# A first projection in hand-written order: unnormalized x, the 1/rms applied at eviction, late constants

## The chip, the cores and the metric

The kernel runs on one core of a Trainium2 chip. The metric is device time in microseconds (us) of one execution; a profile of one further execution gives, for every instruction, its engine, start and duration. The engines are TensorE (PE in the rows; PEld is its weight load), VectorE (DVE), ScalarE (ACT), GpSimd (POOL) and the sync engine (SP), which issues most DMAs.

## The reference, cut to what matters

Two decoder layers over 256 tokens of width 1024. What the change touches is the head of the first layer:

```python
def rmsnorm(x, g):
    xf = x.astype(jnp.float32)
    y = xf * lax.rsqrt(jnp.mean(xf * xf, axis=-1, keepdims=True) + NORM_EPS)
    return (y * g.astype(jnp.float32)).astype(x.dtype)
...
    for layer in range(DEPTH):
        h = rmsnorm(x, pre_norm[layer])
        proj = h @ w_in[layer]
        (hq, hf, hi, hz, nq, kc, vc, ks, vs, kw, vw, ng, nz) = jnp.split(proj, offsets, axis=-1)
```

`nq` (1024 columns) gets a rotary embedding, `hf` (1024 columns) feeds the recurrent group, and the others follow. The rms factor is one number per token, so `(x * g) @ w` scaled by it afterwards gives the same projection.

## The kernel before, in words

All products are made in a split form: every fp32 operand is divided into a high part (a rounded copy, type fp32r) and a low part (the remainder), and one product is three matmuls: high by high, high by low, low by high. So each weight unit costs a ScalarE copy (`whi`, L202) and a VectorE subtraction (`wlo`, L203), both in `convert`, before TensorE may use it.

**The ring.** `plan` lists the weight units, 128 x 1024 numbers each (512 KB), in the order in which they are used: units 0 to 7 for `nq`, 8 to 15 for `hf`, 16 to 19 for `kc`/`vc`, 20 to 23 for `kw`/`vw`/gates (1072 wide), 24 to 27 for the first compressor, 28 to 31 for `ks`/`vs`. `Ring.fill` issues a unit's DMA on SP's queue (L226) into one of five raw buffers; a raw buffer is free again when both halves of the split have read it. Eight split units can be held. `done` releases a unit and fills again; with `lag` set, the conversion is put off by 9 us of a planned clock that `tick` advances with the matmuls.

**The order of work.** The kernel writes down instructions; a scheduler with a cost model then orders them on each engine, and each engine runs its own queue strictly in that order, waiting on semaphores. `later(lag, fn, channel)` plans a step behind the work in hand.

**The head of layer 0 (`layers`, L1075 to L1106).** SP issues the `pre_norm` row, x for tokens 0 to 127 (two halves), the constants table `ct` (identity, rope tables, masks), units 0 and 1, x for tokens 128 to 255, and further units. Four one-row matmuls (L1088) spread the `pre_norm` row over the partitions. `norm_in` squares and sums x (L339), makes 1/rms (L331, L332), multiplies x by it and by the weight (L344), transposes the result by eight TensorE transposes (L351), and splits it into `Hhi` and `Hlo` (L355, L356). Then `a_pair` makes the first projection: for token tile a = 0 and, four units later, for a = 1, six matmuls of 512 columns per unit and tile (`mm_a`, L368 to L370), 96 in all. `nq_evac` takes each finished bank through `rope` (L386 to L393), and 4 us of the planned clock later `turn_q` transposes it (L430) and splits it (L434, L435).

`consts2` loads the second table and six small tensors, clears buffers on GpSimd, transposes twice on TensorE (L293, L294) and makes `posh`, `posl`, `colT`, two masks and `lower_bound` (an exponential, L310) on VectorE and ScalarE. It is written ahead of the first projection.

**What follows.** `hgrn_fast` for c = 0, 1 makes the `hf` projection (`b_group`, `mm_b`, L378 to L380, whose moving operand spans both token tiles) and, behind it, two long scans per c on VectorE. `kcvc`, `kv_w` (whose gates take a sigmoid, L587), `compress` and `kv_s` come next. Three PSUM banks of tag `mm` serve all projections.

## Time and profile before

| | us |
|---|---|
| median of 3 runs | 558.88 (557.16 to 562.67) |
| the profiled execution | 558.97 |
| its span, first to last instruction | 557.2 |

The profile's page gives the busy time of each engine; the timeline lists instructions in order of time, start and duration in us, with the idle time ahead of one in brackets and what ended it; the groups by line give mean durations; the windows give busy time per stretch. PE busy includes time in which a matmul is in flight, so TensorE's rate is read from the steps between the starts of its matmuls.

### The profile page before, as it was taken

Reading aid. Unit: us, or ns where it says so; the run is one execution under the profiler, and the core shown is the slowest. Engines: PE = TensorE matmul, PEld = TensorE weight load, DVE = VectorE, ACT = ScalarE, POOL = GpSimd, SP = SyncE. Lnnn points to the kernel's source line nnn. Section 1 sums busy time; section 2 is a strip of 40 time slices with the busy share of each in tenths; the row PEclk is TensorE's granted clock in tenths of the full one; section 3 lists DMA queues with packets and bytes.
Section 4 is the critical chain, followed back from the end, with each engine's and each line's share of the span. In section 5 each row is a group of like instructions: output and inputs, shape, how many; then the busy total and the mean of one; then the engine's idle time right before and its main releaser. Section 6 shows DMA issues by size and latency. Waiting matters only on the chain.

```text
span 557.2 us, 9821 instructions
## 1 busy us (share of the span) xinstructions
PE 543.8 (98%) x3675; PEld 487.6 (88%) x3675; DVE 398.8 (72%) x883; ACT 333.0 (60%) x632; POOL 9.6 (2%) x18
## 2 busy tenths in 40 slices
PE   7999999999999999999999999989999999999994
PEld 4889998899888989988888999979988888898884
DVE  4887997889777277563687599888987654866422
ACT  6576537865567685562557763677646768746311
POOL 4000000000000001001000000000000000000000
PEclk9999999999999999999999999999999999999998
DMA  8698548965146158566385755697433622956111
GB/s 302 195 314 257 146 127 266 304 193 152 39 117 190 35 166 291 185 191 188 115 262 162 228 154 152 196 302 256 125 101 84 174 85 63 303 172 200 59 38 44
DMA packets 72197, 96.56 MB, mean 173 GB/s; under 512 B 3383, under 2 KB 49357, under 8 KB 72142
## 3 DMA queue, kind: packets, MB, share of 16 engines
q1 hardware_dynamic: 71854, 95.33, 55.2%
q8 instruction: 31, 0.51, 0.4%
q10 hardware_dynamic: 288, 0.52, 0.2%
q14 instruction: 24, 0.20, 0.1%
HBM read 93.75 MB, written 2.10 MB: 172 GB/s over the span
## 4 chain that ended last, share of the span: by engine, by line
PE 88%; DMA 4%; ACT 3%; DVE 2%; issue 1%; SPq 0%; ACTq 0%; DVEq 0%
PE ps_mm L378 10%; PE ps_mm L380 10%; PE ps_mm L379 10%; PE ps_mm L368 9%; PE ps_mm L369 9%; PE ps_mm L370 9%; PE ps_mm L1005 4%; PE ps_mm L1007 4%; PE ps_mm L1006 4%; DMA raw<-in_w_in 2%; ACT whi L202 2%; PE ps_t L668 2%; DMA raw<-in_cmp_w_v 2%; PE ps_s L608 1%; DVE wlo L203 1%
## 5 line engine op out<-in xcount | busy, mean ns | idle before, releaser
L203 DVE TENSOR_TENSOR wlo<-raw,whi 128x1024 fp32r<-128x1024 f32 (+1 forms) x168 | 203.0, 1223 | 60.7 <-ACT whi L202 56.3
L202 ACT CAST whi<-raw 128x1024 fp32r<-128x1024 f32 (+1 forms) x168 | 174.9, 1052 | 87.9 <-PE ps_mm L379 24.5
L378 PE MATMUL ps_mm<-Hhi,whi 128*128 128x256 f32 x448 | 127.5, 285 | 0.0
L380 PE MATMUL ps_mm<-Hhi,wlo 128*128 128x256 f32 x448 | 125.7, 281 | 0.0
L379 PE MATMUL ps_mm<-Hlo,whi 128*128 128x256 f32 x448 | 125.7, 281 | 0.0
L368 PE MATMUL ps_mm<-whi,Hhi 128*128 128x512 f32 (+1 forms) x256 | 102.0, 399 | 0.7 <-ACT Hhi L355 0.7
L370 PE MATMUL ps_mm<-whi,Hlo 128*128 128x512 f32 (+1 forms) x256 | 98.9, 386 | 0.0
L369 PE MATMUL ps_mm<-wlo,Hhi 128*128 128x512 f32 (+1 forms) x256 | 98.8, 386 | 0.0
L379 PEld LDWEIGHTS ps_mm<-Hlo,whi 128*128 128x128 f32 x448 | 84.5, 189 | 0.1
L378 PEld LDWEIGHTS ps_mm<-Hhi,whi 128*128 128x128 f32 x448 | 84.3, 188 | 0.1
L380 PEld LDWEIGHTS ps_mm<-Hhi,wlo 128*128 128x128 f32 x448 | 84.4, 188 | 0.0
L370 PEld LDWEIGHTS ps_mm<-whi,Hlo 128*128 128x128 f32 x256 | 48.7, 190 | 10.3 <-DVE Hlo L356 0.3
L368 PEld LDWEIGHTS ps_mm<-whi,Hhi 128*128 128x128 f32 x256 | 48.9, 191 | 8.5 <-ACT Hhi L355 1.1
L369 PEld LDWEIGHTS ps_mm<-wlo,Hhi 128*128 128x128 f32 x256 | 49.0, 191 | 7.5 <-DVE wlo L203 0.5
L630 ACT ACTIVATE sB<-ps_s,nm 128x256 f32<-128x256 f32 (+1 forms) x40 | 16.9, 428 | 12.2 <-DVE nm L627 11.5
L627 DVE CUSTOM_DVE_ANT_0 ps_s<-ps_s,cm 128x128 f32<-128x128 f32 (+1 forms) x64 | 22.4, 371 | 1.9 <-PE ps_s L610 0.7
L671 DVE TENSOR_TENSOR sB<-ps_t,sB 128x512 fp32r<-128x512 f32 x12 | 8.3, 688 | 20.1 <-ACT sB L670 20.1
L1005 PE MATMUL ps_mm<-whi,sN 128*128 128x512 f32 x48 | 19.0, 397 | 0.0
L1006 PE MATMUL ps_mm<-wlo,Hhi 128*128 128x512 f32 x48 | 18.9, 395 | 0.0
L1007 PE MATMUL ps_mm<-whi,Hlo 128*128 128x512 f32 x48 | 18.9, 395 | 0.0
L1006 PE MATMUL ps_mm<-wlo,sN 128*128 128x512 f32 x48 | 18.9, 394 | 0.0
L1007 PE MATMUL ps_mm<-whi,sN 128*128 128x512 f32 x48 | 18.9, 394 | 0.0
(299 smaller groups left out, 921.0 us busy)
## 6 DMA issues: line engine op xcount, KB each, us to landing
raw<-in_w_in SPq DMA_DIRECT2D x112, 512.0 KB, 4.5
raw<-in_w_out SPq DMA_DIRECT2D x32, 512.0 KB, 4.3
raw<-in_w_in SPq DMA_DIRECT2D x8, 536.0 KB, 4.1
raw<-in_cmp_w_k SPq DMA_DIRECT2D x16, 256.0 KB, 3.4
raw<-in_cmp_w_v SPq DMA_DIRECT2D x16, 256.0 KB, 3.2
sB<-in_x SPq DMA_DIRECT2D x3, 512.0 KB, 3.6
sB<-in_post_norm SPq DMA_DIRECT2D x2, 512.0 KB, 4.8
xs<-sB SPq DMA_DIRECT2D x4, 256.0 KB, 2.0
```

Source lines behind the costliest of these rows:

```text
L202: S.copy(out=hi, in_=raw)
L203: V.tensor_tensor(out=lo, in0=raw, in1=hi.bitcast(F32), op=OP.subtract)
L368: P.matmul(out=ps, lhsT=hh, rhs=wh, start=k == 0, stop=False)
L369: P.matmul(out=ps, lhsT=hh, rhs=wl, start=False, stop=False)
L370: P.matmul(out=ps, lhsT=hl, rhs=wh, start=False, stop=k == KT - 1)
L378: P.matmul(out=ps, lhsT=wh, rhs=hh, start=k == 0, stop=False)
L379: P.matmul(out=ps, lhsT=wh, rhs=hl, start=False, stop=False)
L380: P.matmul(out=ps, lhsT=wl, rhs=hh, start=False, stop=k == KT - 1)
L627: V.tensor_tensor_reduce(out=sb[b], in0=sb[b], in1=mk[b], scale=-1.0, scalar=3e38, op0=OP.add, op1=OP.min, accum_out=nm[:, i, b:b + 1])
L1005: P.matmul(out=ps, lhsT=hi, rhs=wh, start=first, stop=False)
L1006: P.matmul(out=ps, lhsT=hi, rhs=wl, start=False, stop=False)
L1007: P.matmul(out=ps, lhsT=lo, rhs=wh, start=False, stop=last)
```

## The change

The first projection of layer 0 is taken out of `norm_in` and `a_pair` and written as a function `first` inside a block in which the written order is each engine's order.

- x is transposed as it comes, without the norm. The transposes are multiplied by the `pre_norm` column (`whole`), split (`top`, `rest`), and used as the stationary operand of the 96 matmuls (`mm_x`). 1/rms goes into the rope tables and the scale of the eviction (`stats`, `evacuate`).
- For the later projections the normalized `Hhi` and `Hlo` are still needed: 1/rms is turned into a row by one matmul per token tile with a diagonal (`spread`), multiplied in (`product`) and split again (`normal`).
- Units are taken by both token tiles in turn; the weight splits of units 0 to 9 stand at written places, unit 0 in halves.
- Eight and two dummy matmuls of 384 columns (`dummies`) stand ahead of the first product.
- DMAs: the identity and the `pre_norm` column go on ScalarE's queue; SP issues x tile 0, unit 0 (two halves), x tile 1, units 1 and 2, the rest of the table, unit 3.
- `consts2` stands behind `hgrn_fast` for c = 1, with buffers of its own in place of shared ones; its clearing of buffers (`clear`) stays at the start.

```diff
         def convert(self, n):
             while len(self.split) < n:
-                raw, hi, lo, shaped = self.made[len(self.split)]
-                S.copy(out=hi, in_=raw)
-                V.tensor_tensor(out=lo, in0=raw, in1=hi.bitcast(F32), op=OP.subtract)
+                i = len(self.split)
+                if i >= self.early:
+                    self.high(i)
+                    self.low(i)
+                raw, hi, lo, shaped = self.made[i]
                 self.split.append((shaped(hi), shaped(lo)))
...
+    def mm_x(ps, un, u, H, order):
+        last = (u == KT // 2 - 1, order[-1], 1)
+        for j, kind in enumerate(order):
+            for i in range(2):
+                k = 2 * u + i
+                P.matmul(out=ps, lhsT=H[kind[0] == "l"][:, k, :], rhs=un[kind[1] == "l"][:, i, :],
+                         start=(u, j, i) == (0, 0, 0), stop=(True, kind, i) == last)
...
+    def first(ring, general):
...
+        def whole(a, k0, n):
+            ks, o = slice(k0, k0 + n), (k0 % 4) * 128
+            V.tensor_tensor(out=full[a][:, ks, :],
+                            in0=turned[a, k0 // 4][:, o:o + 128 * n].rearrange("p (k t) -> p k t", k=n),
+                            in1=gcol[:, ks, None].to_broadcast([128, n, 128]), op=OP.mult)
+
+        def top(a, k0, n):
+            S.copy(out=H[a][0][:, k0:k0 + n, :], in_=full[a][:, k0:k0 + n, :])
...
+        def product(a):
+            V.tensor_tensor(out=full[a], in0=full[a], in1=rb[a][:, None, 0:128].to_broadcast([128, 8, 128]), op=OP.mult)
+            S.copy(out=Hhi[:, a], in_=full[a])
+
+        def normal(a):
+            V.tensor_tensor(out=Hlo[:, a], in0=full[a], in1=Hhi[:, a].bitcast(F32), op=OP.subtract)
...
+            dummies(8)
+            gp = sb_()
+            P.transpose(out=gp[:, 0:8], in_=grow, identity=ident[0:8, 0:8])
+            V.tensor_copy(out=gcol, in_=gp[:, 0:8])
+            turn_x(0)
+            dummies(2)
+            whole(0, 0, 2)
+            top(0, 0, 2)
+            whole(0, 2, 2)
+            rest(0, 0, 2)
+            ring.high(0, half[0])
+            top(0, 2, 2)
+            ring.high(0, half[1])
+            whole(0, 4, 4)
+            top(0, 4, 4)
+            ring.low(0, half[0])
+            ring.low(0, half[1])
+            ring.fill(6)
+            rest(0, 2, 2)
+            unit(0, 0)
+            turn_x(1)
+            ring.high(1)
+            ring.low(1)
+            ring.fill(7)
+            unit(0, 1)
+            ring.high(2)
+            whole(1, 0, 4)
+            top(1, 0, 4)
+            rest(0, 4, 4)
+            rest(1, 0, 4)
+            whole(1, 4, 4)
+            top(1, 4, 4)
+            ring.low(2)
+            ring.fill(8)
+            rest(1, 4, 4)
+            unit(1, 0, late)
+            unit(1, 1, late)
+            ring.high(3)
+            ring.low(3)
+            unit(0, 2, late)
+            done()
+            unit(1, 2, late)
+            s0 = squares(0)
+            ring.high(4)
+            ring.low(4)
+            unit(0, 3, late)
+            done()
+            s1 = squares(1)
+            ones = slot("B4")[:, 0:128]
+            V.memset(ones, 1.0)
+            ring.high(5)
+            ring.low(5)
+            unit(1, 3, late)
+            done()
+            spread = [stats(0, s0), stats(1, s1)]
+            evacuate(0, 0)
+            unit(0, 4, late)
+            spread[0]()
+            ring.high(6)
+            ring.low(6)
+            evacuate(1, 0)
+            product(0)
+            done()
+            unit(1, 4, late)
+            spread[1]()
+            ring.high(7)
+            ring.low(7)
+            normal(0)
+            unit(0, 5, late)
+            done()
+            unit(1, 5, late)
+            product(1)
+            ring.high(8)
+            ring.low(8)
+            normal(1)
+            unit(0, 6, late)
+            done()
+            unit(1, 6, late)
+            ring.high(9)
+            ring.low(9)
+            unit(0, 7, late)
+            evacuate(0, 1)
+            done()
+            unit(1, 7, late)
+            done()
+            evacuate(1, 1)
+            tick(LQ)
...
         for l in range(DEPTH):
-            a_pair(ring, nq_evac, 8 if l else 4)
+            if l == 0:
+                first(ring, general)
+            else:
+                a_pair(ring, nq_evac, 8)
             rests = []
             for c in range(2):
                 if general:
@@ -1112,6 +1308,8 @@
                     if l and c == 0:
                         nc.gpsimd.memset(ATt, 0.0)
                     rests.append(hgrn_fast(l, c, ring))
+                    if (l, c) == (0, 1):
+                        consts2()
```

## Rows read from the trace of the kernel before

**Rows 1.** The page: busy time, share of the span and instructions of each engine.

```profile
PE 543.8 (98%) x3675; PEld 487.6 (88%) x3675; DVE 398.8 (72%) x883; ACT 333.0 (60%) x632; POOL 9.6 (2%) x18
```

**Rows 2.** Windows: length, then busy us of PE, PEld, DVE, ACT, POOL, granted clock, DMA share, GB/s.

```profile
9.63:37.61 27.98, 27.98 (x118) 22.06 (x119) 23.78 (x50) 20.15 (x29) 0.00 (x0) 1.00 0.83 274
37.61:60.20 22.59, 22.59 (x194) 22.59 (x193) 18.81 (x45) 14.11 (x19) 0.00 (x0) 1.00 0.75 231
60.20:84.10 23.90, 23.90 (x200) 23.90 (x200) 23.03 (x51) 10.31 (x17) 0.00 (x0) 1.00 0.50 147
```

**Rows 3.** Timeline of the head: start us, duration us, engine, line, operation, tiles.

```profile
0.73 0.34 SPq L1084 DMA_DIRECT2D sB<-in_pre_norm  x1
...
1.13 0.83 SPq L157 DMA_DIRECT2D sB<-in_x  x2
...
3.88 0.63 ACT L339 ACTIVATE sA<-sB 128x512 f32<-128x512 f32 x1 [1.66 <-DMA sB<-in_x]
...
6.97 1.97 PE L351 MATMUL ps_t<-ct,sA 128*128 128x128 f32 x8 [0.98 <-DVE sA L344]
8.05 1.05 ACT L202 CAST whi<-raw 128x1024 fp32r<-128x1024 f32 x1 [2.19 <-DMA raw<-in_w_in]
...
9.63 0.79 PE L368 MATMUL ps_mm<-whi,Hhi 128*128 128x512 f32 x1 [0.69 <-ACT Hhi L355]
...
14.57 1.05 ACT L202 CAST whi<-raw 128x1024 fp32r<-128x1024 f32 x1 [0.26 <-DMA raw<-in_w_in]
```

**Rows 4.** Timeline, TensorE: steps between 512-column matmuls, early and settled.

```profile
15.45 0.63 PE L368 MATMUL ps_mm<-whi,Hhi 128*128 128x512 f32 x1
15.88 0.43 PE L369 MATMUL ps_mm<-wlo,Hhi 128*128 128x512 f32 x1
...
26.36 0.40 PE L368 MATMUL ps_mm<-whi,Hhi 128*128 128x512 f32 x1
26.59 0.39 PE L369 MATMUL ps_mm<-wlo,Hhi 128*128 128x512 f32 x1
```

**Rows 5.** Groups by line and form, first 40 us: count, busy us, mean ns.

```profile
L203 DVE TENSOR_TENSOR wlo<-raw,whi 128x1024 fp32r<-128x1024 f32 x15 | 18.1, 1219 | 2.9 <-ACT whi L202 2.9
...
L356 DVE TENSOR_TENSOR Hlo<-ps_t,Hhi 128x512 fp32r<-128x512 f32 x4 | 2.7, 688 | 1.0 <-ACT Hhi L355 1.0
...
L295 DVE CAST posh<-ps_t 128x128 fp32r<-128x128 f32 x1 | 0.3, 292 | 1.4 <-PE ps_t L294 1.4
...
L315 DVE TENSOR_TENSOR lbs<-lbs,lbe 128x8 f32<-128x8 f32 x1 | 0.2, 156 | 0.0
...
L202 ACT CAST whi<-raw 128x1024 fp32r<-128x1024 f32 x16 | 16.6, 1051 | 5.0 <-DMA raw<-in_w_in 2.6 <-PE ps_mm L370 2.4
...
L355 ACT CAST Hhi<-ps_t 128x512 fp32r<-128x512 f32 x4 | 2.2, 586 | 2.2 <-PE ps_t L351 2.2
```

**Rows 6.** Timeline, TensorE: where the next projection begins, and its last `turn_q`.

```profile
37.26 0.60 PE L430 MATMUL ps_t<-ct,st 128*128 128x128 f32 x4
37.61 0.37 PE L378 MATMUL ps_mm<-Hhi,whi 128*128 128x256 f32 x1
...
42.67 0.60 PE L430 MATMUL ps_t<-ct,st 128*128 128x128 f32 x4
```

**Rows 7.** Timeline: VectorE's conversions at 84 us, TensorE's first use of unit 28.

```profile
84.33 2.36 DVE L203 TENSOR_TENSOR wlo<-raw,whi 128x1024 fp32r<-128x1024 f32 x2 [0.26 <-ACT whi L202]
...
87.98 0.39 PE L368 MATMUL ps_mm<-whi,Hhi 128*128 128x512 f32 x1
```

**Rows 8.** Timeline: ScalarE's table loads and the gates' sigmoid.

```profile
31.07 1.28 ACT L310 ACT_TABLE_LOAD   x1
32.36 0.21 ACT L310 ACTIVATE lbe<-lbe 128x16 f32<-128x16 f32 x1
...
44.97 1.28 ACT L726 ACT_TABLE_LOAD   x1
...
82.94 0.19 ACT L587 ACTIVATE gt<-ps_s 128x24 f32<-128x24 f32 x1 [2.33 <-DVE vlo L561]
```

More of the change, by code (lines that the diff above doesn't have):

```diff
@@ L1073, in out_proj, with dummies, turn_x, rest @@
             finish(l, a, y[a], xr[a], gpost, gpre, parts[a])
+    def first(ring, general):
+        H = [[slot("A%d" % (2 * a + i), F32R).rearrange("p (k t) -> p k t", k=8) for i in range(2)] for a in range(NT)]
+        full = [slot("N%d" % a)[:, 0:1024].rearrange("p (k t) -> p k t", k=8) for a in range(NT)]
+        tabs, scales, turned, rb = [], [], {}, {}
+        ps = {}
+        def dummies(n):
+            if not general:
+                for i in range(n):
+                    P.matmul(out=wps[:, 0:384], lhsT=cm3[:, 0:128], rhs=cm3, start=True, stop=True)
+        def turn_x(a):
+            for q in range(2):
+                tp = turned[a, q] = tb()
+                for k in range(4):
+                    P.transpose(out=tp[:, k * 128:(k + 1) * 128],
+                                in_=xr[a][:, (4 * q + k) * 128:(4 * q + k + 1) * 128], identity=ident)
+        def whole(a, k0, n):
[5 more added lines that the diff above has]
+            S.copy(out=H[a][0][:, k0:k0 + n, :], in_=full[a][:, k0:k0 + n, :])
+        def rest(a, k0, n):
+            ks = slice(k0, k0 + n)
+            V.tensor_tensor(out=H[a][1][:, ks, :], in0=full[a][:, ks, :], in1=H[a][0][:, ks, :].bitcast(F32),
+                            op=OP.subtract)
+        def squares(a):
+            ss = small([128, 2], "ss")
+            for q in range(2):
+                S.activation(out=sq[:, q * 512:(q + 1) * 512], in_=xr[a][:, q * 512:(q + 1) * 512], func=AF.Square, accum_out=ss[:, q:q + 1])
+            V.tensor_tensor(out=ss[:, 0:1], in0=ss[:, 0:1], in1=ss[:, 1:2], op=OP.add)
+            return ss
+        def stats(a, ss):
+            r = rstd_of(ss[:, 0:1], D, 1, "r1")
+            sc = small([128, 1], "rsc")
+            tab = small([128, 64], "rtab")
+            V.tensor_scalar(out=sc, in0=r, scalar1=SCALE, scalar2=None, op0=OP.mult)
+            V.tensor_scalar(out=tab, in0=rope_q[a], scalar1=r, scalar2=None, op0=OP.mult)
+            tabs.append(tab)
+            scales.append(sc)
+            rd = small([128, 128], "rd")
+            V.tensor_scalar(out=rd, in0=ident, scalar1=r, scalar2=None, op0=OP.mult)
+            def spread():
+                rb[a] = sb_()
+                P.matmul(out=rb[a][:, 0:128], lhsT=ones, rhs=rd, start=True, stop=True)
+            return spread
+        def product(a):
[3 more added lines that the diff above has]
+            V.tensor_tensor(out=Hlo[:, a], in0=full[a], in1=Hhi[:, a].bitcast(F32), op=OP.subtract)
+        def unit(a, u, order=("hh", "lh", "hl")):
+            if a == 0:
+                units.extend(ring.take(1))
+            if u % 4 == 0:
+                ps[a, u // 4] = mmb()
+            mm_x(ps[a, u // 4], units[u], u % 4, H[a], order)
+        def done():
+            ring.done(1)
+        def evacuate(a, g):
+            nq_evac(a, g, ps[a, g], tabs[a], scales[a])
+        late = ("hh", "hl", "lh")
+        units = []
+        ring.early = 10
+        ring.lag = LAG
+        sq = slot("B1")
+        grow = slot("B0")[0:8, 0:128]
+        gcol = small([128, 8], "gcol", 1)
+        half = [slice(0, 512), slice(512, 1024)]
+        with nullcontext() if general else tc.manual_schedule():
+            if not general:
+                nc.scalar.dma_start(out=ident, in_=A["ct"][:, 0:128])
+            nc.scalar.dma_start(out=grow, in_=A["pre_norm"][0].rearrange("(k p) -> k p", p=128))
+            xr = load_x(0, (0,), 2)
+            ring.fill(1, 2)
+            xr += load_x(0, (1,), 2)
+            ring.fill(3)
+            if not general:
+                V.memset(cm3, 0.0)
+                V.memset(eps_t, EPS)
+                S.activation(out=eps_w, in_=eps_t, func=AF.Sqrt)
+                wps = ob()
+                consts()
+            ring.fill(4)
+            if not general:
+                clear()
+            dummies(8)
[85 more added lines that the diff above has]
+            tick(LQ)
@@ L1077, in layers @@
         lm = None
-        if not general:
-            V.memset(eps_t, EPS)
-            S.activation(out=eps_w, in_=eps_t, func=AF.Sqrt)
-        grow = slot("B0")[0:1, :D]
-        ones = slot("B4")[0:1, 0:128]
-        V.memset(ones, 1.0)
-        nc.sync.dma_start(out=grow, in_=A["pre_norm"][0:1, :])
-        xr = load_x(0, (0,), 2)
-        gpre = [mmb(), mmb()]
-        for q in range(2):
-            P.matmul(out=gpre[q], lhsT=ones, rhs=grow[:, q * 512:(q + 1) * 512], start=True, stop=True)
         if general:
```

48 lines of the change are left out of this document (24 added, 24 removed).

## The prediction, on record before the change ran

> **What bounds the kernel now.** I read the page first, then the windows, then the timeline of the first 45 us. The page shows TensorE busy for 98% of the span [rows 1]. The windows show the same in each early stage, with VectorE beside it at 23.78 of 27.98 us, 18.81 of 22.59 and 23.03 of 23.90 [rows 2]: from the head to 84 us TensorE sets the pace and VectorE is the one engine with little to spare. The timeline then shows what TensorE does not get: its first product starts at 9.63 us, behind the norm and the conversion of unit 0 [rows 3]; and up to 15.88 us a 512-column matmul takes a step of 0.43 us, later one of 0.23 [rows 4]. These are the steps of the two levels, 1.2 and 2.4 GHz; the clock column reads 1.00 throughout this stretch [rows 2], so it is the steps that tell. The next projection begins at 37.61 us, three of the four `turn_q` groups ahead of it, the fourth at 42.67 [rows 6]. I call 37.61 the handover. Everything behind is paced by TensorE, so a handover that is earlier by some time makes the end earlier by as much, unless another engine cannot follow.
>
> **The change part by part.**
>
> *The start.* The `pre_norm` row leaves SP's queue, so x is issued at 0.73 in place of 1.13 us [rows 3] and lands 0.4 earlier, the first half at 3.5 and, by my estimate, the second near 4.3. The norm and the spreading leave the path: today 3.1 us lie between x (3.88) and the first transpose (6.97) [rows 3]. Eight transposes take 1.97 at the low level [rows 3] and end at 6.3. A first product needs half a bank of `whole` (some 0.4, from 0.69 for 512 columns), its `top` (0.35) and a half of unit 0's copy (0.59) [rows 5]; these overlap the transposes, and I get the first matmul at 6.8, 2.8 us earlier than 9.63.
>
> *The weights.* Unit 0 landed at 8.05 with 1.33 MB issued up to it (x tile 0 and the unit at 0.52 each, the table at 0.28), unit 4 at 14.57 with five times 0.52 more, 3.95 MB [rows 3]: 2.62 MB in 6.5 us, 0.40 MB per us. After the change unit 1 has 2.16 MB up to it (both x tiles, units 0 and 1, the identity): 8.05 + 0.83/0.40 - 0.4 = 9.7 us. If all bytes ran at 0.40 from 2.3 us on, it would be 7.7. Between them I take 8.7, and 10.0, 11.8 for units 2 and 3; both ends are kept.
>
> *The clock.* Ten dummies stand ahead of the products. Before, the step fell to 0.23 after 6.3 us of products (9.63 to 15.88) [rows 3, 4]; the dummies run from 1.4 us, so the bounds for the fall are 8 and 16 us. I take 13. Until then VectorE paces the products anyway: on my walk 8 leaves the handover at 36.3 and 16 makes it 37.0.
>
> *VectorE and ScalarE in the written order.* Each engine takes its list as written. I walked both lists by these durations: 1.18 per 1024-column split on VectorE (two in 2.36) [rows 7], 0.69 per 512, 1.05 and 0.59 for ScalarE's copies [rows 5], 0.63 per square [rows 3]. The dates: unit 1 copied at 9.75, its remainder at 10.9; five 512-column pieces of x tile 1 and of tile 0's second half plus unit 2's remainder, and `rest`, up to 15.6; unit 3 at 16.7. Now ScalarE leads: squares, unit 4, squares, unit 5 (1.3 + 1.05 + 1.3 + 1.05 from 15.3) end at 20.0. The factors, a rope, unit 6 and another rope end on VectorE at 25.0. `product(0)` ends at 26.2. Then the two engines wait on each other: ScalarE copies `Hhi` and unit 7 (2 x 1.05, to 28.3), VectorE makes unit 7's remainder, `normal(0)` and `product(1)` (3 x 1.18, to 31.8), ScalarE copies `Hhi` and unit 8 (33.9), VectorE makes unit 8's remainder (35.1) and `normal(1)`: 36.3.
>
> TensorE needs less: 96 steps of 0.23 are 22.3 us, the transposes of x tile 1 and two spreads about 1.5, the low level the rest; its list ends at 33.9. But the moving operand of `mm_b` spans both token tiles, so the second matmul of the next projection waits for `normal(1)`. The handover is 36.3, 1.3 earlier than 37.61. With unit 1 at 9.7 it is 37.3; at 7.7 and an early clock 35.7.
>
> *What moves behind the handover.* TensorE's wait from 33.9 to 36.3 hides two `turn_q` groups; two are left, where one was: +0.35 [rows 6]. The two transposes of the constants come back behind it: +0.25 (two pieces, each less than a `turn_q` group). Their DMAs stand in SP's queue behind the weight loads of `hf`, and the data are first needed by `kcvc`, some 25 us later; SP's issue costs are hidden there. The clearing on GpSimd stays at the start; GpSimd is busy for 9.6 us in all [rows 1].
>
> *VectorE's debt.* At the handover VectorE has split units 0 to 8, nine of them. Today 15 splits start in the first 40 us [rows 5], two of them in the 2.4 us behind the handover, so 13 are done: four more, 4.7 us. One rope more is left (four instructions near 0.29 or less, 1.0), two more `turn_q` remainders (1.4), and the constants: 15 instructions of 0.16 to 0.29 [rows 5], 2.8. Debt 9.9 us. VectorE's idle time up to 84 us is 3.8 + 0.9 [rows 2]; the tightest unit, 28, is ready at 85.5 (one split into the row at 84.33) and used at 87.98 [rows 7], a slack of 2.5. What stays is 2.7 us of TensorE waiting at most, and 0 if the order lets TensorE's needs go first. The window of 60 to 84 us shows VectorE at 96% with no TensorE time lost [rows 2], so I take the lower part: 0.7.
>
> *ScalarE.* The exponential of the lower bound now falls between the sigmoids of `hf` and those of the gates, which need no table load today (82.94) [rows 8]; one load of 1.28 more, hidden, as ScalarE is busy for 10.3 of 23.9 us there [rows 2]. The load row ends at 32.35 and its exponential starts at 32.36 [rows 8]. The Trainium skill, ScalarE: Activation LUTs, section What ACT_TABLE_LOAD costs, adds a drain of about 1.38 us to each switch, and so speaks against the move: by it ScalarE would lose 2.7 us instead of 1.3. The trace does not show that drain. With its cover gone the load adds 1.3 to rival B; by the page it would be 2.7.
>
> *The sum.* -1.3 + 0.35 + 0.25 + 0.7 = 0.0. Against the profiled execution's own time (558.97; span 557.2 and 1.8 around it), which is that of the median 558.88, I predict **559.0 us**: the early start is spent in waiting for VectorE.
>
> **The rivals.**
>
> *A, TensorE's own list sets the handover.* The chain of VectorE and ScalarE is shorter than walked, with unit 1 at 7.7 and the clock up by 8 us; TensorE ends at 31.7, two `turn_q` groups follow, handover 32.4. 558.97 - 5.2 + 0.6 = 554.4. For it: TensorE paces every stage today [rows 2]. Against: the written order makes the engines wait on each other twice at 26 to 34 us. Without any stall (6.8 + 22.3 + 1.2 + 0.7 = 31.0) it would be 553.0.
>
> *B, slower: VectorE becomes the bound from 50 to 88 us.* Its idle time today is waiting for ScalarE's copies and may not be usable; then 9.9 - 2.5 = 7.4 us appear as TensorE waits: 558.97 - 0.7 + 7.4 = 565.7. It decides from the point where the debt exceeds 7.2 us. For it: 23.03 of 23.90. Against: the splits done early today are a lead, not a need.
>
> *C, the dummies do not help.* The step stays at 0.43 until 20 us; TensorE then ends its list at 37.0, and the chain behind it gives a handover of 38.7: +1.1 + 0.6 + 0.7, 561.4. For it: today's first transposes end at 8.94 and the step is 0.43 still at 15.45 [rows 3, 4]. Against: until 16 us VectorE paces the products anyway.
>
> *D, the constants arrive late* behind blocked weight loads, and TensorE stands before their transposes: as long as a unit's load takes, up to 4 us, 563.
>
> **How the numbers follow.** Chances: the forecast 0.52, A 0.22, B 0.14, C 0.07, D 0.05. Range 553.0 to 563.5: it takes in A to its floor, C, D and the lower part of B; the forecast's own range is 557.3 to 561.0 (handover 35.7 to 37.3, debt 0 to 2.7). One per cent, about what a measurement here can tell from no change, is 5.6 us. Faster by that (under 553.3) asks for A at its floor: 0.08. Slower by that (over 564.5) is the upper part of B, and D with a little debt: 0.10. Same: 0.82.
>
> **What would show it.** Right: a first 512-column product near 6.8; steps of 0.23 before 14 us; TensorE's wait for `normal(1)` of some 2 us around 34 to 36; the first 256-column matmuls in a dense row at 36.3; VectorE without idle time from there to 80. Wrong: no wait at the handover (A), TensorE waits between 60 and 92 us (B), steps of 0.43 past 16 us (C), a wait at the transposes of the constants (D).

## The result, and the profile after

The changed kernel takes 564.35 us (median; 564.05 to 565.92), the kernel before 558.84 us beside it: a ratio of 1.0090 with a 95% interval of 1.0072 to 1.0108. The forecast was 559.0. The profiled execution took 564.38 us with a span of 561.5; before, 558.97 and 557.2.

The page of the changed kernel, busy time by engine, as in [rows 1]:

```profile
PE 544.0 (97%) x3686; PEld 487.7 (87%) x3686; DVE 403.9 (72%) x898; ACT 336.7 (60%) x637; POOL 9.2 (2%) x17
```

TensorE is busy for the same time as before (543.8) in a span that is 4.3 us longer, so it stands longer; slow matmuls count as busy and do not show in this figure. The windows of the changed kernel, columns as in [rows 2], show where time goes:

```profile
6.34:37.93 31.59, 26.57 (x118) 20.25 (x118) 22.55 (x43) 18.85 (x31) 0.00 (x0) 1.00 0.70 225
37.93:41.40 3.47, 3.47 (x16) 3.47 (x17) 3.44 (x10) 3.47 (x6) 0.00 (x0) 0.51 0.88 222
41.40:60.20 18.80, 18.80 (x162) 18.80 (x161) 17.30 (x27) 14.49 (x18) 0.00 (x0) 1.00 0.89 276
60.20:86.00 25.80, 25.80 (x217) 25.80 (x216) 25.80 (x78) 12.31 (x17) 0.00 (x0) 1.00 0.54 153
```

Two things are new. In the first projection TensorE is busy for 26.57 of 31.59 us, where before it was busy all the time; and behind the handover the granted clock is 0.51 for 3.47 us (about the lower of its two levels, called half clock below), in which 16 matmuls of 256 columns take a step of 0.217 us instead of 0.117. The last line shows a third: VectorE is busy for every one of 25.80 us up to 86. TensorE's timeline (start us, duration us, line, tiles, idle time before and its releaser) at the start and at the handover:

```profile
4.11 1.09 PE L1116 MATMUL ps_t<-ct,sB 128*128 128x128 f32 x8
5.04 0.49 PE L1110 MATMUL ps_o<-cm 128*128 128x384 bf16 x2
6.34 0.50 PE L394 MATMUL ps_mm<-whi,sA 128*128 128x512 f32 x1 [0.81 <-ACT whi L201]
...
33.67 1.04 PE L454 MATMUL ps_t<-ct,st 128*128 128x128 f32 x8
35.53 0.39 PE L402 MATMUL ps_mm<-Hhi,whi 128*128 128x256 f32 x1 [0.82 <-ACT whi L201]
37.93 0.56 PE L403 MATMUL ps_mm<-Hlo,whi 128*128 128x256 f32 x1 [2.01 <-DVE Hlo L1162]
```

The first product starts at 6.34 us (9.63 before, [rows 3]). TensorE's products end at 33.67 and two `turn_q` groups follow; then it waits twice, at last for `normal(1)` (L1162). VectorE's timeline shows why that is late:

```profile
24.41 0.23 DVE L314 CAST mask<-m 128x128 uint8<-128x128 f32 x1 [1.10 <-DMA m<-in_ct]
...
26.34 0.22 DVE L315 CAST cm<-m 128x128 bf16<-128x128 f32 x1
...
29.96 1.23 DVE L205 TENSOR_TENSOR wlo<-raw,whi 128x1024 fp32r<-128x1024 f32 x1 [2.06 <-ACT whi L201]
31.10 1.22 DVE L1162 TENSOR_TENSOR Hlo<-sN,Hhi 128x1024 fp32r<-128x1024 f32 x1
32.24 1.22 DVE L1158 TENSOR_TENSOR sN<-sN,ps_s 128x1024 f32<-128x1024 f32 x1
35.51 1.23 DVE L205 TENSOR_TENSOR wlo<-raw,whi 128x1024 fp32r<-128x1024 f32 x1 [2.06 <-ACT whi L201]
36.65 1.22 DVE L1162 TENSOR_TENSOR Hlo<-sN,Hhi 128x1024 fp32r<-128x1024 f32 x1
```

The scheduler put the two casts of the second set of constants (L314, L315) into the written order, ahead of a rope, unit 6 and `product(0)`; VectorE stood 1.10 us for their load. Then come two waits of 2.06 us for ScalarE's copies.

The same matmuls dated in both traces show where the time is lost:

| matmul | before | after | difference |
|---|---|---|---|
| second of the next projection (L379, now L403) | 37.81 | 37.93 | +0.1 |
| 13th of L378, now L402 | 42.0 | 43.7 | +1.7 |
| first of `compress` (L492, now L516) | 84.2 | 86.6 | +2.4 |
| first of L531, now L555 (transposes of `kst`, a tile of VectorE) | 103.44 | 106.58 | +3.1 |
| 37th of L845, now L869 (recurrent group, layer 0) | 141.90 | 145.17 | +3.3 |
| 128th of L845, now L869 (layer 1) | 411.60 | 415.46 | +3.9 |
| end of the last one | 549.69 | 553.60 | +3.9 |

To this come 0.4 us between the last matmul and the end of the span, and 1.1 us around the span (the execution's time less the span: 2.88 against 1.77).

### The profile page after: what moved, and what is told of

It is laid out like the page before. It is cut to its first block, busy times and chain, and to the rows that moved or that the text cites. A ratio compares the mean times of both kernels' runs of the same rounds, so it can differ in the third digit from the quotient of the medians.

```text
span 561.5 us, 9856 instructions
## 1 busy us (share of the span) xinstructions
PE 544.0 (97%) x3686; PEld 487.7 (87%) x3686; DVE 403.9 (72%) x898; ACT 336.7 (60%) x637; POOL 9.2 (2%) x17
## 4 chain that ended last, share of the span: by engine, by line
PE 72%; DVE 12%; ACT 5%; DMA 5%; issue 5%; SPq 0%; ACTq 0%; DVEq 0%
PE ps_mm L403 7%; PE ps_mm L402 7%; PE ps_mm L404 7%; PE ps_mm L384 7%; PE ps_mm L385 7%; PE ps_mm L386 7%; PE ps_mm L1029 4%; PE ps_mm L1031 4%; PE ps_mm L1030 4%; DVE wlo L205 4%; ACT whi L201 3%; DMA raw<-in_cmp_w_v 2%; PE ps_t L692 2%; PE ps_s L632 1%; PE ps_s L965 1%
## 5 line engine op out<-in xcount | busy, mean ns | idle before, releaser
L205 DVE TENSOR_TENSOR wlo<-raw,whi 128x1024 fp32r<-128x1024 f32 (+2 forms) x169 | 203.5, 1217 | 61.6 <-ACT whi L201 59.2
L201 ACT CAST whi<-raw 128x1024 fp32r<-128x1024 f32 (+2 forms) x169 | 174.9, 1047 | 78.9 <-PE ps_mm L403 18.0
L402 PE MATMUL ps_mm<-Hhi,whi 128*128 128x256 f32 x448 | 128.3, 286 | 0.8 <-ACT whi L201 0.8
L403 PE MATMUL ps_mm<-Hlo,whi 128*128 128x256 f32 x448 | 126.7, 283 | 2.0 <-DVE Hlo L1162 2.0
L384 PE MATMUL ps_mm<-whi,Hhi 128*128 128x512 f32 (+1 forms) x224 | 88.0, 393 | 0.0
L403 PEld LDWEIGHTS ps_mm<-Hlo,whi 128*128 128x128 f32 x448 | 85.3, 190 | 2.3 <-DVE Hlo L1162 2.2
L402 PEld LDWEIGHTS ps_mm<-Hhi,whi 128*128 128x128 f32 x448 | 85.3, 190 | 1.2 <-ACT whi L201 1.1
L385 PE MATMUL ps_mm<-wlo,Hhi 128*128 128x512 f32 (+1 forms) x224 | 85.1, 380 | 0.0
L386 PE MATMUL ps_mm<-whi,Hlo 128*128 128x512 f32 (+1 forms) x224 | 85.0, 379 | 0.0
L384 PEld LDWEIGHTS ps_mm<-whi,Hhi 128*128 128x128 f32 x224 | 42.2, 188 | 6.1 <-issue 0.4
L385 PEld LDWEIGHTS ps_mm<-wlo,Hhi 128*128 128x128 f32 x224 | 42.3, 189 | 5.5
L654 ACT ACTIVATE sB<-ps_s,nm 128x256 f32<-128x256 f32 (+1 forms) x40 | 16.9, 429 | 12.2 <-DVE nm L651 11.5
L394 PE MATMUL ps_mm<-whi,sA 128*128 128x512 f32 x64 | 18.6, 402 | 2.9 <-ACT whi L201 2.3
L1029 PE MATMUL ps_mm<-whi,sN 128*128 128x512 f32 x48 | 19.0, 397 | 0.0
L1029 PE MATMUL ps_mm<-whi,Hhi 128*128 128x512 f32 x48 | 18.9, 394 | 0.0
```

What stands on the lines that cost most here:

```text
L201: S.copy(out=hi[:, s], in_=raw[:, s])
L205: V.tensor_tensor(out=lo[:, s], in0=raw[:, s], in1=hi[:, s].bitcast(F32), op=OP.subtract)
L384: P.matmul(out=ps, lhsT=hh, rhs=wh, start=k == 0, stop=False)
L385: P.matmul(out=ps, lhsT=hh, rhs=wl, start=False, stop=False)
L386: P.matmul(out=ps, lhsT=hl, rhs=wh, start=False, stop=k == KT - 1)
L402: P.matmul(out=ps, lhsT=wh, rhs=hh, start=k == 0, stop=False)
```

## The experiments

The theory after the two traces: VectorE's queue ahead of the handover, with the constants in it, delays `normal(1)`, and the wait makes the clock fall. The rival: the time is lost on another engine or later on, and the handover does not set it. Each ratio below is to the kernel before run beside the experiment (medians from 557.77 to 559.00 us), so experiments are compared by ratios rather than by times.

### c_late: the mask constants behind the first projection

```diff
-        m2 = small([128, 256], "m2", 1)
+        m2 = slot("N1")[:, 0:256]
```

> The changed kernel, but the tile of the mask constants (m2) shares the memory of the unnormalized x (N1), so that its load cannot be issued before the last product has been read; its two casts leave VectorE's queue ahead of the handover. Theory 1 (VectorE's queue ahead of the handover sets it): the 1.1 us that VectorE stood for m2 and the two casts (0.45 us) go, normal(1) ends near 36.4 us instead of 37.87, the first dense matmul behind it starts there, 562.9 us if the clock still falls afterwards, 561.3 if the shorter wait keeps it up. Theory 2 (a later stage takes the time anyway, the constants only moved the wait): 564.3 us within 0.3.

Measured: 562.82 us, 1.0087 (1.0067 to 1.0108) of the time before. In the timelines VectorE's last subtraction and TensorE's matmul behind it:

```profile
35.41 1.22 DVE L1162 TENSOR_TENSOR Hlo<-sN,Hhi 128x1024 fp32r<-128x1024 f32 x1
```

```profile
34.28 0.39 PE L402 MATMUL ps_mm<-Hhi,whi 128*128 128x256 f32 x1
36.68 0.39 PE L403 MATMUL ps_mm<-Hlo,whi 128*128 128x256 f32 x1 [2.01 <-DVE Hlo L1162]
```

`normal(1)` starts 1.24 us earlier, as theory 1 has it, and the handover is 36.68. TensorE still waits, and the granted clock is 0.59 from 36.68 to 40.83. In the traces the 37th L869 is 1.2 us earlier than in the changed kernel; the ratio of the times does not tell the two kernels apart.

### c_pad: TensorE kept busy in the wait

```diff
             unit(1, 7, late)
+            if not general:
+                for i in range(12):
+                    P.matmul(out=wps, lhsT=H[1][0][:, 0, :], rhs=H[1][0][:, 0:4, :].rearrange("p k t -> p (k t)"),
+                             start=True, stop=True)
             done()
```

> The changed kernel with 12 more matmuls of 512 columns (0.232 us each, 2.8 us) whose result nobody reads, between the last matmul of the first projection (33.7 us) and the q transposes, in the stretch where TensorE waits for the normalized remainder of tile 1. Theory 1 (the half clock from 38.0 to 41.4 us comes of that wait and costs 1.5 us): the handover stays at 37.9 us, the granted clock stays at full level behind it, the 256-column step is 0.117 us at once, 562.8 us. Theory 2 (the clock falls for another reason, or the time is lost anyway): 564.3 us, and the step is 0.21 us behind the handover as before.

Measured: 563.40 us, 1.0117 (1.0083 to 1.0151). The windows ahead of the handover and behind it:

```profile
33.70:37.90 4.20, 4.20 (x24) 3.55 (x23) 2.45 (x3) 2.95 (x4) 0.00 (x0) 1.00 0.11 30
37.90:41.40 3.50, 3.50 (x31) 3.50 (x30) 3.41 (x9) 3.50 (x6) 0.00 (x0) 1.00 0.83 248
```

The clock stays at 1.00, and 31 matmuls run where 16 did. So, by these two traces, the fall behind the handover came of the wait, and at 42 us TensorE is 1.5 us ahead of the changed kernel. But nothing of it is left later. TensorE's timeline in two stretches:

```profile
85.97 0.34 PE L516 MATMUL ps_s<-whi,sN 128*68 128x256 f32 x1 [0.66 <-ACT gt L611]
...
106.81 0.26 PE L555 MATMUL ps_t<-ct,kst 15*128 15x15 f32 x2 [1.92 <-DVE kst L417]
```

TensorE now waits at L516 and longer at L555 (1.02 before the edit), and the 37th L869 is at 145.43 us, not earlier than 145.17. Theory 1 had the price of the half clock right (1.5 us) and its worth wrong: the rival, that the handover does not set the time, got its first support.

### c_order: copies of the next units ahead of the products' copies

```diff
             evacuate(1, 0)
+            ring.high(7)
             product(0)
...
-            ring.high(7)
             ring.low(7)
+            ring.high(8)
             normal(0)
...
             product(1)
-            ring.high(8)
+            ring.high(9)
             ring.low(8)
             normal(1)
...
-            ring.high(9)
             ring.low(9)
```

> The changed kernel with another order between the copies of the units and the products: ScalarE copies unit 7 ahead of product(0)'s copy, units 8 and 9 ahead of the copies that VectorE waits for, and VectorE's subtractions follow accordingly; the constants stay where they are. Theory 1 (two waits of 2.06 us of VectorE for ScalarE's copies set the handover): normal(1) ends at 34 to 35 us instead of 37.87, TensorE's wait shrinks from 3.5 us in sum to about 1, the clock stays up, 560 us (559.5 to 561.5). Theory 2 (other waits of VectorE take their place, or what is won is lost by 105 us): 563.5 to 564.3 us.

Measured: 561.57 us, 1.0077 (1.0058 to 1.0097). Both waits of 2.06 us are gone, `normal(1)` starts at 32.91 instead of 36.65, TensorE does not wait at the handover (second matmul at 35.26) and the clock stays up. At 80 us TensorE is 1.8 us ahead of the kernel before. Then, in the timeline of all engines:

```profile
82.10 1.22 DVE L205 TENSOR_TENSOR wlo<-raw,whi 128x1024 fp32r<-128x1024 f32 x1
...
82.25 0.38 PE L576 MATMUL ps_t<-ct,kst 128*128 128x128 f32 x2
83.23 0.42 DVE L585 TENSOR_TENSOR vlo<-ps_s,vhi 128x256 fp32r<-128x256 f32 x1
...
83.68 0.19 ACT L611 ACTIVATE gt<-ps_s 128x24 f32<-128x24 f32 x1 [2.57 <-DVE vlo L585]
...
83.93 0.33 PE L516 MATMUL ps_s<-whi,sN 128*68 128x256 f32 x1 [1.30 <-ACT gt L611]
```

Read from below: TensorE waits for ScalarE's gates (`gt`), ScalarE for VectorE's `vlo` copy (L585, the low part of the split `v`), and VectorE comes to that copy out of a queue without a pause. The lead of 1.8 us is given back here but for 0.2 (the first L516 starts at 83.93, the first L492 before at 84.17). VectorE is the second bound. The handover is theory 1's; by its ratio the time is nearer theory 2's, in which what is won is lost by 105 us.

### c_both: both edits together

> The changed kernel with both edits of two earlier runs: the mask constants' load behind the last use of N1, and the copies of units 7 to 9 ahead of the products' copies. Theory 1 (behind the handover VectorE's queue is the second bound: in the run with the new order alone TensorE came to the first L516 1.6 us earlier than in the kernel before relative to its own waits and stood 1.57 us there for VectorE and ScalarE): taking the 1.55 us of m2's wait and casts out of VectorE's queue shortens that wait to 0 to 0.5 us, the handover is at 34.3 us, L516 starts near 82.6 us, the time is that of the kernel before within 0.4% (0.996 to 1.000). Theory 2 (the wait at L516 is that of a transfer or of ScalarE's table load and not of VectorE's backlog): L516 starts at 83.9 us again, 1.004 to 1.008 of the time before.

Measured: 560.49 us, 1.0020 (0.9998 to 1.0042). The handover is at 34.49, but theory 1 failed on the rest: the `vlo` copy starts at 83.56, no earlier than 83.23. VectorE had the 1.55 us back and stood for other things, 1.16 us for ScalarE's rope ahead of 34.80 and 1.04 us for ScalarE's copy ahead of 48.50. TensorE is 2.6 us ahead of the kernel before at 78 us and waits 1.79 us at L516 (2.06 from start to start); the time lies between the two theories. The windows show the clock behind that wait:

```profile
82.20:84.25 2.05, 0.26 (x3) 0.02 (x2) 1.77 (x3) 0.24 (x2) 0.00 (x0) 1.00 0.48 184
84.25:88.00 3.75, 3.75 (x19) 3.75 (x20) 3.26 (x8) 3.75 (x7) 0.00 (x0) 0.55 0.51 153
```

### c_gp: six remainders on GpSimd

```diff
+GPLOW = (11, 14, 17, 20, 23, 26)
...
-            V.tensor_tensor(out=lo[:, s], in0=raw[:, s], in1=hi[:, s].bitcast(F32), op=OP.subtract)
+            (nc.gpsimd if i in GPLOW else V).tensor_tensor(out=lo[:, s], in0=raw[:, s], in1=hi[:, s].bitcast(F32), op=OP.subtract)
```

(on c_both)

> As the run with both edits, and the remainders of six weight units (11, 14, 17, 20, 23 and 26) subtracted on GpSimd instead of VectorE: 6 times 1.15 us taken out of VectorE's queue between the handover and L516. Theory 1 (VectorE's backlog sets L516 and part of the wait at L555): no wait over 0.3 us ahead of L516, L555 at 102.5 us or earlier, 0.5 to 1.5 us less than the run with both edits. Theory 2 (GpSimd's subtraction takes so much longer than VectorE's 1.22 us that TensorE waits for those units): 1 to 3 us more than the run with both edits, with waits of TensorE at L402 to L404 behind those units.

Measured: 566.05 us, 1.0112 (1.0075 to 1.0150). GpSimd's and VectorE's timelines show more than a slow engine:

```profile
53.44 3.73 POOL L206 TENSOR_TENSOR wlo<-raw,whi 128x1072 fp32r<-128x1072 f32 x1 [2.34 <-ACT whi L202]
54.78 3.47 DVE L206 TENSOR_TENSOR wlo<-raw,whi 128x1024 fp32r<-128x1024 f32 x1
```

```profile
59.65 2.49 POOL L206 TENSOR_TENSOR wlo<-raw,whi 128x1072 fp32r<-128x1072 f32 x1 [2.48 <-ACT whi L202]
59.68 2.50 DVE L808 TENSOR_TENSOR km<-rc,ok 128x16 f32<-128x16 f32 x1
```

While GpSimd subtracts, VectorE's subtraction takes 3.47 us instead of 1.22, and one of 16 columns takes 2.50 us instead of 0.17: each ends only after GpSimd's (57.17 and 62.14) has. So the work that was moved still took VectorE's time: its busy time up to the first `vlo` copy is 75.4 us, where c_both has 72.1 with six subtractions more. TensorE then stood 4.91 us ahead of 80.94 for a tile of VectorE (`sN`, L503). The Trainium skill, SBUF — State Buffer, section SBUF: two separate sides, states this: VectorE and GpSimd share a pair of ports as an exclusive lock, held for a whole instruction, and a VectorE operation with two inputs from SBUF is shut out by a GpSimd operation that reads SBUF. The trace agrees, with 3.47 and 2.50 us. Theory 2 had the sign, not the mechanism; and theory 1 could not be tested in this way.

### c_sched: the same operations in the scheduler's order

```diff
-        with nullcontext() if general else tc.manual_schedule():
+        with nullcontext():
```

> The changed kernel with the order inside the first projection left to the scheduler instead of written out; the operations are the same. Theory 1 (the written order costs what the waits of VectorE ahead of the handover cost, and a scheduler that orders by due time would avoid them): normal(1) ends at 34 to 36 us, 1.002 to 1.006 of the time before. Theory 2 (the written order is what makes the start fast): the products of the first units begin 1 to 3 us later, 1.010 to 1.015. Theory 3 (order is not the point, the extra operations are): 1.008 to 1.010 as the changed kernel.

Measured: 557.20 us, 0.9968 (0.9947 to 0.9989): 0.3% faster than the kernel before, with the interval below 1. Theory 1 was right in kind and too timid. The windows:

```profile
12.00:33.47 21.47, 21.47 (x100) 17.46 (x99) 21.09 (x34) 15.69 (x20) 0.00 (x0) 1.00 0.86 279
33.47:60.00 26.53, 26.53 (x228) 26.53 (x227) 24.38 (x53) 19.52 (x26) 0.00 (x0) 1.00 0.78 243
60.00:84.00 24.00, 24.00 (x202) 24.00 (x201) 23.12 (x66) 12.09 (x20) 0.00 (x0) 1.00 0.45 137
```

From 12 to 84 us TensorE is busy throughout, and VectorE is busy for 21.09 of 21.47 us ahead of the handover. ScalarE's timeline shows one likely reason, which no run tried alone: the squares stand at the very start, while the first units are on their way:

```profile
3.89 0.63 ACT L1136 ACTIVATE sB<-sB 128x512 f32<-128x512 f32 x1 [0.60 <-DMA sB<-in_x]
...
8.53 0.61 ACT L1136 ACTIVATE sB<-sB 128x512 f32<-128x512 f32 x1
```

### c_nodum and s_nodum: without the dummy matmuls, in either order

```diff
-            dummies(8)
...
-            dummies(2)
```

> The changed kernel without the ten dummy matmuls at the start. Theory 1 (the first unit's landing near 9.5 us and the copies behind it set the first 14 us, and the clock's date matters little: in three runs it rose at 3.9, 9.6 and 10.1 us and the product of unit 1 began at 11.2 to 11.6 us all the same): unit 3 at 16 to 17 us as with them, the time within 0.5 us of the changed kernel's (1.008 to 1.011 of the time before). Theory 2 (without them the clock stays at half until 14 to 17 us and every product of the first units takes 0.43 us): 1.5 to 3 us more than the changed kernel, 1.012 to 1.015.

> The changed kernel with the scheduler's order inside the first projection, without the ten dummy matmuls. Theory 1 (the clock's date does not matter, since the second unit's copies set the restart of TensorE at 11.2 us): within 0.7 us of the run with them, 0.996 to 0.998 of the time before. Theory 2 (with no wait of VectorE ahead of the handover TensorE is the bound from 11 us on, and products at 0.43 us up to 12 to 16 us cost time): 1 to 2.5 us more, 0.998 to 1.001.

Measured: in the written order 564.39 us, 1.0084 (1.0057 to 1.0110), which the intervals do not tell from 1.0090. The one trace does not confirm that the dummies are worth nothing there: it is of the slowest of nine executions (561.78 to 566.39), and in it the handover is at 39.09 instead of 37.93 and the last matmul ends 2.1 us later. In the scheduler's order 558.80 us, 1.0003 (0.9993 to 1.0013), against 0.9968 with them; in the traces the last matmul ends 1.6 us later and the handover is at 35.05 instead of 33.68. So the dummies are worth some 0.35% where TensorE does not wait for VectorE at the handover; where it does, the times show no worth, within some 2 us.

### b_dummy: dummy matmuls in the kernel before

```diff
+            zero = cp.tile([128, 384], BF, name="zero")
+            V.memset(zero, 0.0)
...
+            wps = ob()
+        def dummies(n):
+            if not general:
+                for i in range(n):
+                    P.matmul(out=wps[:, 0:384], lhsT=zero[:, 0:128], rhs=zero, start=True, stop=True)
+        dummies(4)
...
+        dummies(3)
...
+        dummies(2)
```

> The kernel before with 9 bf16 matmuls of 384 columns on a zero tile, whose result nobody reads, at the start of TensorE's queue (about 1.1 to 4 us), and nothing else of the change. Theory 1 (the clock alone is worth the 2.6 us of the 13 matmuls at 0.43 us): the clock rises near 4 us instead of 15.95, the step is 0.23 us from the first product on, handover 35.0 instead of 37.61, 556.2 us. Theory 2 (with the clock up, the units' copies on ScalarE and VectorE set the pace to 16 us): handover at 37.0 to 37.6, 558.3 to 558.8 us. Theory 3 (the dummies delay the broadcast of the norm's weights by 1.7 us and the clock does not rise): 560.4 us.

Measured: 558.63 us, 1.0012 (0.9995 to 1.0029), beside a time before of 557.77. All nine ran first, at 0.32 us each. TensorE's timeline shows the step of 0.43 up to 13.34 us (15.88 before, [rows 4]):

```profile
12.94 0.57 PE L368 MATMUL ps_mm<-whi,Hhi 128*128 128x512 f32 x1
13.34 0.40 PE L369 MATMUL ps_mm<-wlo,Hhi 128*128 128x512 f32 x1
13.58 0.40 PE L370 MATMUL ps_mm<-whi,Hlo 128*128 128x512 f32 x1
```

The handover was 0.9 us earlier and the 37th L845 1.6 us earlier; both went again in layer 1, where a wait of 1.63 us was followed by a granted clock of 0.59 from 371.0 to 375.2. None of the three theories fits whole.

### s_early: the second set of constants at the start

```diff
             if not general:
                 clear()
+                consts2()
...
-                    if (l, c) == (0, 1):
-                        consts2()
```

(on c_sched)

> The changed kernel with the scheduler's order inside the first projection, and the second set of constants loaded and prepared at the start, ahead of the first projection, instead of behind it. Theory 1 (the late constants are a gain of VectorE's time ahead of the handover): casts, remainder and the small chain of the lower bound (some 20 instructions, 2 to 3 us of VectorE) stand ahead of the handover, which comes 1 to 3 us later than the 33.5 us of the run with late constants, 1 to 3 us more in the time. Theory 2 (VectorE has room there or pays the same behind the handover, as its work up to the first vlo copy is the same): within 0.7 us of that run (0.996 to 0.998 of the time before).

Measured: 568.07 us, 1.0161 (1.0144 to 1.0178). This does not price the late constants either. The dummies read the tile that L315 writes, and now stood behind it in TensorE's queue with the transposes of x behind them, as its timeline shows:

```profile
9.98 0.80 PE L1153 MATMUL ps_s<-rd,sB 128*128 128x128 f32 x2 [0.98 <-DVE rd L1149]
13.73 1.76 PE L1110 MATMUL ps_o<-cm 128*128 128x384 bf16 x5 [2.96 <-DVE cm L315]
```

### c_less and s_more: less and more work on VectorE

```diff
             raw, hi, lo, shaped = self.made[i]
+            if i in (14, 20):
+                nc.gpsimd.memset(lo.bitcast(F32), 0.0)
+                return
```

That is c_less, on c_both; s_more, on c_sched, repeats the subtraction:

```diff
             raw, hi, lo, shaped = self.made[i]
-            V.tensor_tensor(out=lo[:, s], in0=raw[:, s], in1=hi[:, s].bitcast(F32), op=OP.subtract)
+            for again in range(2 if i in (14, 20) else 1):
+                V.tensor_tensor(out=lo[:, s], in0=raw[:, s], in1=hi[:, s].bitcast(F32), op=OP.subtract)
```

> As the run with both edits, with less work on VectorE: the remainders of units 14 and 20 (1.15 us each) are not subtracted; GpSimd writes zeros there instead (that part of the computation is left out). Theory 1 (between the handover and the vlo copy that releases the first L516 VectorE is never idle, so that copy's date is the sum of VectorE's work and waits before it): the first vlo copy starts 2 to 2.5 us earlier, near 81.3 us instead of 83.56, TensorE's wait of 2.06 us ahead of L516 goes to 0.3 us or less, the granted clock stays at full level at 84 us, 1.5 to 3.5 us less than the run with both edits. Theory 2 (ScalarE's table load, the transfers or the place of the copy in the queue set the date): the wait of about 2 us stays and the time is within 0.7 us of the run with both edits.

> The changed kernel with the scheduler's order inside the first projection, with more work on VectorE: the remainders of units 14 and 20 are subtracted twice (2 times 1.15 us more, behind the handover). In the eleven earlier experiments and the two kernels the first matmul of line L869's fourth dozen (before: L845) came 58.8 to 60.2 us behind the start of VectorE's first vlo copy, though that copy's date ran from 79.96 to 89.03 us. Theory 1 (the sum of VectorE's work and waits up to that copy sets the pace of the first layer's front): the handover stays at 33.5 us, the copy starts near 82.3 us instead of 79.96, the dozen at 141.3 instead of 138.98, the time is 2.3 us more than that of the run without the repetition, 1.000 to 1.002 of the time before. Theory 2 (TensorE is the bound there, and the copy's date only follows it): both dates and the time within 0.7 us of that run, 0.996 to 0.998.

Measured: with less work 560.74 us, 1.0029 (1.0009 to 1.0048); with more 557.78 us, 0.9980 (0.9960 to 0.9999), against 0.9968. In both the `vlo` copy moved by less than the work: 1.1 us earlier (82.47) for 2.3 us less, 1.0 us later (80.92) for 2.3 us more. VectorE had waits to fill: c_sched's wait of 1.03 us ahead of 45.56 is 0.17 in s_more, and in c_less the waits grew by 0.9. The 37th L869 moved with the copy (1.2 us earlier, 1.3 later), so theory 1 holds in kind and with about half of its size. In c_less that did not reach the end: a wait of 1.63 us ahead of 372.88 was followed by half clock, and 2.0 to 3.1 us lay around the span, where c_both has 1.6.

### All traces side by side

Dates in us of the matmul behind the handover, of VectorE's first `vlo` copy (L561 before, L585 after) and of the 37th L869 (L845 before); VectorE's busy time up to that copy (by the windows; its instructions overlap by some 0.09 us, so the durations of its rows add up to more) and its idle time, which is the rest.

| kernel | handover | busy | idle | `vlo` | 37th L869 | behind `vlo` |
|---|---|---|---|---|---|---|
| c_sched | 33.68 | 71.7 | 8.3 | 79.96 | 138.98 | 59.0 |
| s_more | 33.91 | 73.6 | 7.3 | 80.92 | 140.26 | 59.3 |
| s_nodum | 35.05 | 71.8 | 9.5 | 81.31 | 140.53 | 59.2 |
| b_dummy | 36.90 | 66.9 | 14.6 | 81.55 | 140.30 | 58.8 |
| c_less | 34.73 | 70.1 | 12.4 | 82.47 | 141.69 | 59.2 |
| before | 37.81 | 67.0 | 15.5 | 82.49 | 141.90 | 59.4 |
| c_order | 35.26 | 72.1 | 11.1 | 83.23 | 142.24 | 59.0 |
| c_both | 34.49 | 72.1 | 11.5 | 83.56 | 142.92 | 59.4 |
| c_late | 36.68 | 70.6 | 14.2 | 84.77 | 143.93 | 59.2 |
| c_pad | 37.91 | 70.6 | 14.7 | 85.27 | 145.43 | 60.2 |
| after | 37.93 | 70.7 | 15.1 | 85.80 | 145.17 | 59.4 |
| c_nodum | 39.09 | 70.6 | 17.6 | 88.16 | 147.60 | 59.4 |
| s_early | 43.08 | 72.9 | 15.5 | 88.43 | 147.55 | 59.1 |
| c_gp | 34.85 | 75.4 | 13.6 | 89.03 | 148.29 | 59.3 |

Over 9 us of dates the last column stays between 58.8 and 60.2; the distance from the handover to the 37th L869 runs from 103.4 to 113.4. So the front of layer 0 keeps step with VectorE's date and not with the handover. That two dates go together does not say which leads. In every trace the `vlo` copy starts without a pause of VectorE, 0.7 to 3.8 us after its input `vhi` is ready, so VectorE's own queue, its work and its earlier waits, sets its date. TensorE waits for it at L516 in c_order, c_both, c_less, c_pad, s_more and c_gp; in the other eight, the changed kernel and the kernel before among them, TensorE comes to L516 without a wait, and which engine leads there is not shown. Some 20 us on, at L555 (L531 before), TensorE waits 0.1 to 1.9 us for VectorE's `kst` in all but b_dummy and c_both.

What is certain by the times is less than what the traces show: in the written order no single edit moves the ratio beyond the intervals, both edits together (c_both) do, and so does the scheduler's order.

The windows up to the handover and from there to the `vlo` copy, columns as in [rows 2], of the kernel before, the changed kernel and c_sched:

```profile
0.00:37.81 37.81, 33.89 (x131) 24.99 (x132) 26.42 (x57) 25.15 (x38) 5.93 (x15) 1.00 0.81 269
37.81:82.49 44.68, 44.68 (x378) 44.68 (x376) 40.58 (x89) 23.07 (x32) 0.00 (x0) 1.00 0.63 190
```

```profile
0.00:37.93 37.93, 30.86 (x137) 22.45 (x137) 24.34 (x49) 21.41 (x35) 5.58 (x14) 1.00 0.70 225
37.93:85.80 47.87, 47.87 (x389) 47.87 (x390) 46.33 (x112) 30.27 (x40) 0.00 (x0) 0.96 0.70 205
```

```profile
0.00:33.68 33.68, 31.23 (x137) 24.01 (x137) 27.68 (x50) 24.27 (x37) 5.58 (x14) 1.00 0.84 282
33.68:79.96 46.28, 46.28 (x391) 46.28 (x390) 44.02 (x111) 27.81 (x38) 0.00 (x0) 1.00 0.64 198
```

Up to the `vlo` copy the change costs VectorE 3.7 us of work (70.7 against 67.0), and the written order leaves it idle for about as long as before (15.1 against 15.5). The scheduler's order has 4.7 us more work than before (71.7) and 7.2 us less idle time (8.3), so its copy starts 2.5 us earlier.

## Why the prediction was wrong, point by point

**The start: right.** First product 6.34 (forecast 6.8), unit 1's copy from 9.50 on (forecast from 8.7 to 9.75), unit 3's remainder done at 17.26 (16.7). Steps of 0.23 came with the first products in the profiled execution, better than the 13 us taken; rival C was wrong. What this was worth in the written order, the times of c_nodum do not show.

**The walk up to the handover: right but for what was not on the list.** The chain `Hhi`, unit 7, `normal(0)`, `product(1)`, `Hhi`, unit 8, `normal(1)` ran as walked, with the two waits between the engines. It ended at 37.93 instead of 36.3. (I set the 36.3 against 37.61, the first matmul of the next projection; the one that waits for `normal(1)` is the second, which was at 37.81 before.) In c_late, with the masks' casts out of the way, it ended at 36.68. The step that failed here is that of the constants: I counted their VectorE work behind the handover and looked only at SP's issue and at `kcvc`'s need; two casts and the 1.10 us for their load stood in VectorE's queue ahead of `product(0)`. Rival D looked for this wait on TensorE, where it was not: the transposes at 63.0 us waited for nothing.

**The clock behind the wait: missing from the sum.** I let TensorE wait from 33.9 to 36.3 us for `normal(1)` and charged only the wait. The half clock behind it cost 1.5 us more at 42 us. c_pad shows the cause, and also that this term alone did not decide: without it the 37th L869 was no earlier.

**The rule behind the sum, and VectorE's debt: the step that decided.** "A handover that is earlier by some time makes the end earlier by as much, unless another engine cannot follow": in the written order the exception was the rule. I had read 23.03 of 23.90 us in [rows 2], reckoned a debt of 9.9 us at the handover, and let all but 0.7 us of it (at most 2.7) vanish in 4.7 us of VectorE's idle time and 2.5 us of slack at unit 28. That term, 0.7, is the one that was mis-sized. Measured by VectorE's first `vlo` copy it is 3.3 us (85.80 against 82.49). The windows above give its parts: behind the handover VectorE has 46.33 us of work where it had 40.58, a debt of 5.8 and not 9.9; of the 4.1 us of idle time there 1.5 remain, so 2.6 us were filled, and 3.2 stayed (0.1 more is the handover's). The debt was smaller than reckoned (17 split instructions stood behind the handover where 14 had, three more and not four, and short instructions overlap, so that they take less time than their durations add up to); the relief was smaller still, as I had taken idle time as free to be filled. The debt had grown ahead of the handover, where VectorE idled 13.6 us instead of 11.4: the three waits shown make 5.2 us of that, where before those from 22 us on made 2.5. In the changed kernel itself the two losses hide each other: TensorE comes to L516 2.4 us later than before of itself and finds VectorE ready, so that rival B's sign, a wait of TensorE between 60 and 92 us, does not appear. It appears as soon as TensorE's own loss is taken away (c_pad, c_order, c_both). This is rival B's mechanism at less than half of B's price of 7.4 us. That VectorE's side decided rests on those traces: c_late took 1.2 us out of VectorE's queue and the 37th L869 came 1.2 us earlier, while c_pad gave TensorE 1.5 us and it did not.

**What moved behind the handover: right.** Two `turn_q` groups were left (45.34 and 46.02), the constants' transposes cost 0.2 us. ScalarE's load for the exponential (1.28 us at 65.18) was followed by a wait of 3.03 us for VectorE's `lbe`, which I had not foreseen; whether it cost anything was not tried.

**What stays open.** Of the 5.5 us, 3.3 are there by 145 us. Another 0.6 arise in layer 1, where the experiments have between -0.2 and 1.0 without an edit there (1.8 and 2.4 in b_dummy and c_less, whose clock fell there), 0.4 between the last matmul and the end of the span, and the rest around the span. This last part is 2.0 to 2.9 us in every run of the changed kernel and 1.8 in the kernel before; it was 1.5 to 1.7 in c_order and c_both, 1.8 in c_sched, and 2.0 to 3.1 in c_late, c_pad, c_nodum and c_less. I found nothing that tells these groups apart; no run tried it.

**Operations and order.** The same operations in the scheduler's order make the kernel 0.3% faster than before, the fastest version tried. Against c_sched it is the written order that costs the 1.2%; the operations cost VectorE time in both, and c_sched pays for it out of idle time.

## What to carry to other kernels

Where two engines are both over 95% busy in a window, follow both to the first place at which one waits for the other, and sum each one's work and waits up to there, with the overlap of its instructions taken off: here the later date was the price, and a lead of the other engine was given back. An order written by hand has to be walked with all that the scheduler may put between its lines, and with one piece of lead wherever two engines hand tiles to and fro; here the scheduler did it 1.2% better. A wait of TensorE has to be charged with the slow matmuls behind it too, and a help like dummy matmuls showed a worth only where TensorE was the bound.

## What the runs showed of the hardware

The granted clock fell behind waits of TensorE of 2.01 us (the changed kernel, c_late, c_nodum), 1.79 (c_both) and 1.63 (b_dummy, c_less): 0.50 to 0.59 over the next 3.5 to 6.1 us; and behind the 4.91 us of c_gp, 0.62 over the next 5.1. It stayed at 1.00 behind waits of 1.92 us in c_pad and 1.45 in c_order. So a short wait can cost almost as much again (1.5 us behind the 2.01), and not each one does. At the start, with the same dummies, the step of 0.43 us did not appear in the products of the changed kernel and c_order, but lasted to near 10 us in c_late and c_pad: a date of the clock taken from one execution does not hold for the next. And GpSimd's subtraction on tiles in SBUF held up VectorE's for as long as it ran (c_gp).
